# A hybrid decoder layer on one core: four banks begun ahead, filler dealt anew, late constants held back, the last tile by halves

## The chip, the cores and the metric

The kernel runs on one core of one Trainium2 chip. The metric is the device time of one execution in microseconds (us). TensorE (PE) multiplies, VectorE (DVE), ScalarE (ACT) and GpSimd (POOL) do elementwise work, SyncE (SP), ACT and POOL issue DMAs. L12 is line 12 of the kernel before.

## What is computed

One pre-norm decoder layer, x of 512 tokens by 1024 features in float32:

```python
h = rms_norm(x, g_mix)
qa, ka, va, qb, kb, vb, gl = split(h @ w_in)      # 1024 x 4352
ya = swa_sink_attention(rms(qa), rms(ka), va)     # 8 heads, window 128, banded 128-blocks
yb = rms_norm(diff_attention(rms(qb), rms(kb), vb))  # 4 heads, A1 - lam*A2, causal
mixed = sigmoid(gA) * (ya @ w_br_a) + sigmoid(gB) * (yb @ w_br_b)
x = x + mixed @ w_o
u = causal_dwconv3(rms_norm(x) @ w_up)            # 1024 x 5632
x = x + (silu(u_g) * u_v) @ w_down                # 2816 x 1024
```

Both attentions add a relative-position bias that is looked up from a small table.

## The kernel before, in words

**Products.** Each float32 operand is split into a rounded high part and a remainder, and `mm3` (L170 to L174) makes a product of three matmuls: high x high, one operand's remainder, the other's remainder. One `mm3` of 512 columns is called a step here. Weights come from DRAM in units of 128x1024 (`wall`), in the order of `worder`. `split_unit` (L125 to L133) loads a unit on SP (L128), makes `whi` on ACT (L131) and `wlo` on DVE, or on POOL for the units in `pooled` (L132, L158). `wunit(u)` hands out unit u and has everything up to `AHEAD` = 1 unit further loaded and split. There are three raw, three `whi` and three `wlo` buffers.

**Who sets the order.** PE's order is the order of the program text. ACT, DVE and POOL are ordered by a planner from its own estimate of costs, except in the start (L300 to L332), where ACT and DVE too follow the text. Every engine executes its queue in order.

**Start.** SP loads x in eight slices of 128 features (L257) and the first weight units; ACT makes the high part of each x slice (L286), DVE the remainder (L287). POOL issues three loads of constants that are needed later: `relb` (16 KB) and `oneh` (48 KB), from which `bias_vectors` makes the bias, and the part of `cst` behind column `C_HEAD` (216 KB). PE runs eight warming matmuls (L245), then the q projection slice by slice (L348, then `mm3`).

**Attention with filler.** PE would wait at every turn between scores, softmax and value product, so the list `FILL` deals steps of other products (gates, projections, branch products) from a stream `fs` into the gaps: so many steps at each place. `q`, `k`, `k2` stand around the transposes of q and k; `s1`, `s2`, `s3` in unit i of the window attention, after `swa_score(i)`, `swa_trans(i-1)` and `swa_av(i-2)`; in the differential attention (16 units: 4 heads by 4 blocks) `a` after `diff_score`, `c` after `diff_av` and `b` after `diff_trans`. `diff_rms(h)` (norm of a head's output on DVE and ACT, L754 to L761) runs at unit `r[h]` and `diff_out(h)` (transposes on PE, L767, then L768, L769) at unit `o[h]`, both cut at 16, followed by `d[h]` and `e[h]` steps.

**Branch B and w_o.** `br_b_early` begins the first `EARLY` of eight output chunks of `yb @ w_br_b` with three of their four steps each; each holds a PSUM bank. After the attention the last step of these is done (L875 to L883) and the other chunks are made whole by `full`. `mix` then takes each chunk: DVE adds and multiplies (L868, L869), ACT makes the high part (L871), POOL the remainder (L872). `late` (L847) starts the first two chunks of `mixed @ w_o`, six of eight steps each, then the other two; `wunit(U_WO)` and `wunit(U_WO + 1)` are called there, after all mixes.

**Feed-forward.** 44 chunks of w_up, each followed by `conv` on ACT and DVE (L956 to L971); the down product is done by a seven-product scheme (`product`), whose last product T4 ends in two tiles of 128x512, added to the residual on DVE (L1085) and stored by ACT's queue (L1053).

Of the kernel before, what the change touches and what calls it, by code (L numbers as in the profile page):

```python
# [16 lines left out]
ALU = mybir.AluOpType  # L17
AX = mybir.AxisListType

P = 128  # L20
S = 512
# [24 lines left out]
C_HEAD = C_LAM  # L46
# [5 lines left out]
U_QA, U_KV, U_DA, U_VB, U_DB = 0, 4, 6, 10, 14  # L52
U_BRA = 18
U_GATE = 22
U_BRB = 38
U_WO = 42
U_UP = 50
# [8 lines left out]

FILL = dict(r=[5, 9, 13, 16], o=[6, 10, 14, 16], e=[5, 1, 1, 40], kv=4, up=3, warm=8, q=7, k=19, k2=4,
            s1=[0, 3, 0, 3, 2, 4, 4, 0, 0, 3], s2=[2, 3, 0, 5, 1, 7, 5, 5, 0, 0],  # L70
            s3=[3, 0, 2, 5, 6, 2, 2, 6, 0, 1], p0=4, p1=3, p2=10, ud=6, pd=[8, 9], f=[9, 0],
            a=[6, 1, 7, 8, 10, 2, 0, 5, 0, 2, 7, 3, 6, 0, 0, 5],
            b=[6, 2, 4, 4, 2, 7, 2, 1, 2, 2, 0, 0, 1, 4, 2, 2], c=[3, 0, 0, 0, 2, 0, 0, 0, 2, 1, 0, 0, 1, 0, 0, 0],
            d=[1, 0, 0, 5], v0=4)
AHEAD = 1
EARLY = 5


@with_exitstack
def tile_decoder_layer(ctx: ExitStack, tc: tile.TileContext, x4, wall, cst_d, relb_d, oneh_d, xn_d, out):  # L80
    nc = tc.nc
# [19 lines left out]
    def xg_slot():  # L101
        return slot("xg", 16)
# [10 lines left out]
    def pj():  # L113
        return psum.tile([P, S], F32, tag="ps", name=nm("pj"))

    def at():
        return psum.tile([P, S], F32, tag="ps", name=nm("at"))


    cst = const.tile([P, C_N], F32, name="cst")  # L120
# [4 lines left out]
    def split_unit(i, width, eng):  # L125
        raw = wraw.tile([P, 1024], F32, tag="raw", name=nm("raw"))
        src = wall[i] if i < U_N else tsum[(i - U_N) // 6][(i - U_N) % 6]
        nc.sync.dma_start(raw[:, :width], src[:, :width])  # L128
        hi = whip.tile([P, 1024], F32R, tag="hi", name=nm("whi"))
        lo = whip.tile([P, 1024], F32R, tag="lo", name=nm("wlo"))  # L130
        nc.scalar.activation(hi[:, :width], raw[:, :width], AF.Copy)  # L131
        eng.tensor_tensor(lo[:, :width], raw[:, :width], hi[:, :width].bitcast(F32), ALU.subtract)  # L132
        return hi, lo  # L133
# [21 lines left out]
                                 (U_DB, 4), (U_GATE + 8, 8), (U_BRB, 4), (U_WO, 8), (U_UP, 2 * NF), (U_DN, 0))  # L155
              for i in range(n)]
    worder += [U_DN + 6 * op + u for op in DN_ORDER for u in range(6)]
    pooled = {u + i for u, n in ((U_DA, 4), (U_VB, 4), (U_DB, 4), (U_BRA, 4), (U_GATE, 16), (U_BRB + 3, 1)) for i in range(n)}  # L158
    units = {}
    wnext = [4]  # L160

    def wunit(u):
        while wnext[0] < len(worder) and wnext[0] <= worder.index(u) + AHEAD:
            v = worder[wnext[0]]
            width = 512 if v >= U_DN and (v - U_DN) % 6 == 5 else 1024
            units[v] = split_unit(v, width, nc.gpsimd if v in pooled else nc.vector)
            wnext[0] += 1
        return units.pop(u)

    def mm3(ps, a, b, start, stop, skip=False):  # L170

        nc.tensor.matmul(ps, a[0], b[0], start=start, stop=False, skip_group_check=skip)  # L172
        nc.tensor.matmul(ps, a[0], b[1], start=False, stop=False, skip_group_check=skip)  # L173
        nc.tensor.matmul(ps, a[1], b[0], start=False, stop=stop, skip_group_check=skip)  # L174
# [68 lines left out]
    ps = at()  # L243
    for i in range(FILL["warm"]):
        nc.tensor.matmul(ps, zero[:, :P], zero, start=True, stop=True)  # L245

    nc.scalar.dma_start(cst[:, :C_HEAD], cst_d[:, :C_HEAD])
    relb = at1.tile([N_BUCKETS, P], F32, tag="s", name="relb", bufs=3)
    nc.gpsimd.dma_start(relb, relb_d)
    oneh = at1.tile([N_BUCKETS, TOEP], F32, tag="o", name="oneh", bufs=3)  # L250
    nc.gpsimd.dma_start(oneh, oneh_d)
    xr = []
    for k in range(NK):
        xr.append(g_slot(F32))
# [1 line left out]
    def load_x(k, c=slice(0, S)):  # L256
        nc.sync.dma_start(xr[k][:, c], x4[:, k, c])  # L257
# [23 lines left out]
    def split_x(k, c=slice(0, S)):  # L281
        if c.start == 0:
            xg.append((xg_slot(), xg_slot()))
        h, l = [t[:, c] for t in xg[k]]
        gcol = cst[:, C_GMIX + k:C_GMIX + k + 1]
        nc.scalar.activation(h, xr[k][:, c], AF.Copy, scale=gcol)  # L286
        return nc.vector.scalar_tensor_tensor(l, xr[k][:, c], gcol, h.bitcast(F32), ALU.mult, ALU.subtract)  # L287
# [4 lines left out]
    def load_xnat(i):  # L292
        nc.sync.dma_start(xnat[i], xn_d[2 * i:2 * i + 2].rearrange("t p d -> p t d"))

    def square_xnat(t):
        v = xnat[t // 2][:, t % 2, :]
        return nc.scalar.activation(v, v, AF.Square, accum_out=rsum[:, t:t + 1])

    make_identity(nc, ident)
    start = ExitStack()  # L300
# [21 lines left out]
    for kp in range(1, NK // 2):  # L322
        load_x(2 * kp)
        split_x(2 * kp)
        units[U_QA + kp] = split_unit(U_QA + kp, 1024, nc.vector)
        load_x(2 * kp + 1)
        x_split = split_x(2 * kp + 1)
    for i in range(2):
        load_xnat(i)
    for t in range(NT):  # L330
        square_xnat(t)
    start.close()  # L332
    nc.gpsimd.dma_start(cst[:, C_HEAD:], cst_d[:, C_HEAD:])

    def project(u0, width, banks, lead=False):
# [151 lines left out]
    def cut(w, k):  # L487
        return [w[i][:, k * P:(k + 1) * P] for i in range(2)]
# [26 lines left out]
    class Stream:  # L515
# [18 lines left out]
        def fill(self, n):  # L534
            while n > 0 and self.step():
                n -= 1
# [7 lines left out]
    def fill(name, i=None):  # L544
        fs.fill(FILL[name] if i is None else FILL[name][i])

# [229 lines left out]
    def brb_unit(c):  # L776
        if c // 2 not in wb:
            wb[c // 2] = wunit(U_BRB + c // 2)
        return wb[c // 2]
# [3 lines left out]
    def br_b_early():  # L783
        for c in range(EARLY):
            w = brb_unit(c)
            ps = pj()
            for k in range(3):
                mm3(ps, cut(w, 4 * (c % 2) + k), yb[k], start=k == 0, stop=False)
                yield
            brb_banks.append((ps, w))  # L790
# [13 lines left out]
    for i in range(len(todo) + 1):  # L804
        if i < len(todo):
            h, b = todo[i]
            if i == FILL["ud"]:
                fs.until("db")
            for h1 in (2, 3):
                if i == FILL["pd"][h1 - 2]:  # L810
                    qkt[h1] = diff_parts(zt[2], h1 - 2)
# [3 lines left out]
        if i > 0:  # L815
            for u, hb in enumerate(todo):
                if u < len(todo) - 1 and max(u + 2, FILL["v0"]) == i:
                    fs.until("vb")
# [4 lines left out]
            if i == len(todo):  # L823
                diff_av(*todo[-1])
        for step, at_unit in ((diff_rms, FILL["r"]), (diff_out, FILL["o"])):
            for h1 in range(4):
# [19 lines left out]

    def late(u0, grp, cuts, xs, evac):  # L847

        ws = [wunit(u0 + c) for c in range(grp)]
        banks = [pj() for _ in range(grp)]  # L850
        for k0, k1 in zip(cuts, cuts[1:]):
            for ps, w in zip(banks, ws):
                for k in range(k0, k1):
                    mm3(ps, cut(w, k), xs[k], start=k == 0, stop=k == NK - 1)
        for c, ps in enumerate(banks):
            evac(c, ps)

    def full(c, w, off, nk, xs, evac):
        ps = pj()
        for k in range(nk):  # L860
            mm3(ps, cut(w, off + k), xs[k], start=k == 0, stop=k == nk - 1)
        evac(c, ps)
# [13 lines left out]
    for c, (ps, _) in enumerate(brb_banks):  # L876
        for part in last[c]:
            nc.tensor.matmul(ps, part, yb[3][0], start=False, stop=False)
    for c in range(EARLY, 8):
        brb_unit(c)  # L880
    for c, (ps, _) in enumerate(brb_banks):
        nc.tensor.matmul(ps, last[c][0], yb[3][1], start=False, stop=True)
        mix(c, ps)  # L883
    for c in range(EARLY, 8):
        full(c, brb_unit(c), 4 * (c % 2), 4, yb, mix)


# [87 lines left out]
    steps = [(op, u) for op in DN_ORDER for u in range(6)]  # L975
# [12 lines left out]
    first = []  # L988
    for c in range(2):
        w = wunit(U_UP + c)  # L990
# [40 lines left out]
    def product(op, banks, first):  # L1031

        n0 = steps.index((op, 0))
        for u in range(6):
            n = n0 + u
            w = wunit(U_DN + 6 * op + u)
            if n + 1 < len(steps) and n > 0:
                split_left(n + 1)
            a = lefts.pop(n)
            for t in range(2):  # L1040
                for j in range(2 if u < 5 else 1):
                    mm3(banks[t], [a[i][:, 256 * j + P * t:256 * j + P * t + P] for i in range(2)],
                        [w[i][:, 512 * j:512 * j + 512] for i in range(2)],
                        start=first and u == 0 and j == 0, stop=u == 5, skip=not first)
            if op == DN_ORDER[0] and u > 0:
                for i in range(8 * (u - 1) // 5, 8 * u // 5):
                    x1_natural(i // 2, i % 2)
# [4 lines left out]
    def store(i, j, t, v):  # L1052
        nc.scalar.dma_start(out[(2 * i + t) * P:(2 * i + t + 1) * P, j * S:(j + 1) * S], v)  # L1053

    chain, n5 = [at(), at()], [at(), at()]
    product(R11, chain, True)
    p1, us, n5s, ws = [], [], [], []
# [11 lines left out]
    p2 = [at(), at()]  # L1069
# [12 lines left out]
    product(T4, chain, False)  # L1082
    for t in range(2):
        v = x1n[2 * (2 + t)]
        nc.vector.tensor_tensor(v, chain[t], v, ALU.add)  # L1085
        store(1, 0, t, v)


def _bucket_onehot():
# [82 lines left out]
```

## Time and profile before

| | |
|---|---|
| median of 3 runs | 712.83 us |
| lowest, highest | 712.62, 714.18 us |
| the profiled execution: its time | 711.81 us |
| its span, first to last instruction | 710.0 us |
| mean granted TensorE clock | 0.995 |
| PE busy | 690.0 us (97%) |
| DVE, ACT, POOL busy | 486.1, 371.3, 196.8 us |

The profiled execution is 1.8 us longer than its span, and 1.0 us shorter than the median. A row of a timeline gives start, length, engine, line, operation, tiles and, in brackets, the idle time of that engine before it and what ended it.

### The profile page before, as it was taken

The numbers are of one execution on the slowest core, as the hardware profiler recorded it, in microseconds if no ns is written. First come the engines' busy times: TensorE is split into PE (matmuls) and PEld (weight loads), VectorE is DVE, ScalarE is ACT, GpSimd is POOL, SyncE is SP. The second block draws the span as 40 slices with busy tenths as digits, with TensorE's granted clock in tenths as the row PEclk, the third lists the DMA queues.
The fourth block names the chain that finished last, engine by engine and source line by source line (L and its number), as shares of the span: only waits on it lengthen the run. The fifth ranks groups of instructions, "written<-read, shape, count | busy, mean of one in ns | idle before, by whom it ended". The sixth has DMA issues, their size and how long they took to land.

```text
span 710.0 us, 9146 instructions
## 1 busy us (share of the span) xinstructions
PE 690.0 (97%) x3220; PEld 568.2 (80%) x3220; DVE 486.1 (68%) x978; ACT 371.3 (52%) x690; POOL 196.8 (28%) x168
## 2 busy tenths in 40 slices
PE   7999999999999989989999999999999999999997
PEld 5897888778888867768888788888888888888886
DVE  5686786567517787585438868777767677788783
ACT  5537777865336867434325344343334334766661
POOL 2144254533347310283300514332123120100000
PEclk9999999999999999999999999999999999999999
DMA  8672112112232211035422896997986432566773
GB/s 306 260 267 90 60 60 90 59 60 90 70 109 69 80 60 61 30 108 163 144 90 79 281 297 190 324 292 196 266 237 158 138 107 87 162 192 188 228 219 107
DMA packets 28493, 107.86 MB, mean 152 GB/s; under 512 B 3652, under 2 KB 3936, under 8 KB 27936
## 3 DMA queue, kind: packets, MB, share of 16 engines
q1 hardware_dynamic: 21568, 73.67, 31.0%
q0 software_dynamic: 4816, 18.92, 11.9%
q10 hardware_dynamic: 2064, 14.70, 5.5%
q8 instruction: 25, 0.41, 0.2%
q14 instruction: 20, 0.16, 0.1%
HBM read 105.16 MB, written 29.64 MB: 190 GB/s over the span
## 4 chain that ended last, share of the span: by engine, by line
PE 87%; DVE 5%; ACT 5%; issue 1%; DMA 1%; SPq 0%; ACTq 0%; DVEq 0%
PE pj L174 22%; PE pj L172 22%; PE pj L173 22%; PE at L173 5%; PE at L174 5%; PE at L172 5%; DVE g L869 1%; PE at L472 1%; PE at L471 1%; DMA g<-in_x_dram 1%; DVE wlo L132 1%; PE at L626 1%; ACT p L711 1%; DVE g L868 1%; PE at L442 1%
## 5 line engine op out<-in xcount | busy, mean ns | idle before, releaser
L131 ACT ACTIVATE whi<-raw 128x1024 fp32r<-128x1024 f32 x135 | 139.4, 1035 | 152.7 <-PE pj L173 99.1
L172 PE MATMUL pj<-xg,whi 128*128 128x512 f32 x480 | 189.5, 395 | 0.0
L174 PE MATMUL pj<-xg,wlo 128*128 128x512 f32 x480 | 187.7, 391 | 1.2 <-DVE wlo L132 1.2
L173 PE MATMUL pj<-xg,whi 128*128 128x512 f32 x480 | 187.6, 391 | 0.0
L132 DVE TENSOR_TENSOR wlo<-raw,whi 128x1024 fp32r<-128x1024 f32 x102 | 124.8, 1226 | 35.5 <-ACT whi L131 35.0
L132 POOL TENSOR_TENSOR wlo<-raw,whi 128x1024 fp32r<-128x1024 f32 x33 | 79.4, 2411 | 113.8 <-ACT whi L131 108.2
L174 PEld LDWEIGHTS pj<-xg,wlo 128*128 128x128 f32 x480 | 90.4, 188 | 20.6 <-DVE wlo L132 1.7
L172 PEld LDWEIGHTS pj<-xg,whi 128*128 128x128 f32 x480 | 90.5, 189 | 18.1 <-ACT whi L131 0.4
L173 PEld LDWEIGHTS pj<-xg,whi 128*128 128x128 f32 x480 | 90.4, 188 | 17.9
L172 PE MATMUL pj<-whi,xg 128*128 128x512 f32 (+1 forms) x156 | 59.2, 379 | 1.8 <-ACT xg L286 1.8
L956 DVE TENSOR_TENSOR u<-pj,rbc 128x512 f32<-128x512 f32 x44 | 30.2, 689 | 42.2 <-PE pj L174 42.1
L174 PE MATMUL pj<-whi,xg 128*128 128x512 f32 (+1 forms) x156 | 58.3, 374 | 0.1
L173 PE MATMUL pj<-wlo,xg 128*128 128x512 f32 (+1 forms) x156 | 58.0, 372 | 0.0
L172 PE MATMUL at<-whi,xg 128*128 128x512 f32 x146 | 57.3, 393 | 0.0
L174 PE MATMUL at<-whi,xg 128*128 128x512 f32 x146 | 57.0, 390 | 0.0
L173 PE MATMUL at<-wlo,xg 128*128 128x512 f32 x146 | 56.9, 390 | 0.0
L959 ACT ACTIVATE yc<-u,cst 128x512 f32<-128x512 f32 x44 | 35.3, 806 | 9.4 <-DVE u L956 9.1
L963 DVE SCALAR_TENSOR_TENSOR yc<-u,cst,yc 128x511 f32<-128x511 f32 x44 | 35.6, 810 | 2.9 <-ACT yc L959 2.9
L969 ACT ACTIVATE yc<-yc 128x512 f32<-128x512 f32 x22 | 13.9, 632 | 44.6 <-DVE yc L964 44.2
L172 PEld LDWEIGHTS pj<-whi,xg 128*128 128x128 f32 x156 | 29.9, 192 | 7.0 <-ACT xg L286 2.2
L964 DVE SCALAR_TENSOR_TENSOR yc<-u,cst,yc 128x510 f32<-128x510 f32 x44 | 34.1, 777 | 1.3
L174 PEld LDWEIGHTS pj<-whi,xg 128*128 128x128 f32 x156 | 29.8, 191 | 5.7 <-DVE xg L287 0.5
(251 smaller groups left out, 1152.0 us busy)
## 6 DMA issues: line engine op xcount, KB each, us to landing
raw<-in_w_dram SPq DMA_DIRECT2D x108, 512.0 KB, 3.4
tsum<-in_w_dram POOLq DMA_DIRECT2D x24, 512.0 KB, 11.8
raw<-tsum SPq DMA_DIRECT2D x20, 512.0 KB, 3.7
tsum<-in_w_dram ACTq DMA_DIRECT2D x12, 512.0 KB, 6.9
tsum<-tsum ACTq DMA_DIRECT2D x12, 512.0 KB, 6.4
scr<-scr POOLq DMA_DIRECT2D x1, 2304.0 KB, 11.3
xnat<-in_xn_dram SPq DMA_DIRECT2D x2, 1024.0 KB, 9.4
tmp<-in_x_dram POOLq DMA_DIRECT2D x8, 256.0 KB, 3.3
```

The source lines that it names most:

```text
L131: nc.scalar.activation(hi[:, :width], raw[:, :width], AF.Copy)
L132: eng.tensor_tensor(lo[:, :width], raw[:, :width], hi[:, :width].bitcast(F32), ALU.subtract)
L172: nc.tensor.matmul(ps, a[0], b[0], start=start, stop=False, skip_group_check=skip)
L173: nc.tensor.matmul(ps, a[0], b[1], start=False, stop=False, skip_group_check=skip)
L174: nc.tensor.matmul(ps, a[1], b[0], start=False, stop=stop, skip_group_check=skip)
L442: nc.tensor.transpose(ps[:, t * P:(t + 1) * P], zs[t][:, c0:c0 + P], ident)
L471: nc.tensor.matmul(ps, q[:, qsl], kh[:, ksl], start=True, stop=False)
L956: nc.vector.tensor_tensor(u, ps, rbc2, ALU.mult)
L959: i = nc.scalar.activation(y, u, AF.Identity, bias=cst[:, C_CB + ch:C_CB + ch + 1], scale=cw[2])
L963: nc.vector.scalar_tensor_tensor(y[:, 1:S], u[:, 0:S - 1], cw[1], y[:, 1:S], ALU.mult, ALU.add)
L964: nc.vector.scalar_tensor_tensor(y[:, 2:S], u[:, 0:S - 2], cw[0], y[:, 2:S], ALU.mult, ALU.add)
L969: nc.scalar.activation(yg, yg, AF.Silu)
```

## The change

It sets `EARLY` to 4, deals the filler anew, moves `diff_out(1)` from unit 10 to unit 12, makes DVE split `U_BRB + 3` and POOL split `U_UP + 4` to `U_UP + 6`, has the three POOL loads of constants wait for a DVE memset that stands after the split of x slice 3, takes `wunit(U_WO)` (and with it the load and split of `U_WO + 1`) before chunk 6 of branch B, and computes, adds and stores the very last tile in two halves of 256 columns, the second on SP's queue.

```diff
-FILL = dict(r=[5, 9, 13, 16], o=[6, 10, 14, 16], e=[5, 1, 1, 40], kv=4, up=3, warm=8, q=7, k=19, k2=4,
-            s1=[0, 3, 0, 3, 2, 4, 4, 0, 0, 3], s2=[2, 3, 0, 5, 1, 7, 5, 5, 0, 0],
-            s3=[3, 0, 2, 5, 6, 2, 2, 6, 0, 1], p0=4, p1=3, p2=10, ud=6, pd=[8, 9], f=[9, 0],
-            a=[6, 1, 7, 8, 10, 2, 0, 5, 0, 2, 7, 3, 6, 0, 0, 5],
-            b=[6, 2, 4, 4, 2, 7, 2, 1, 2, 2, 0, 0, 1, 4, 2, 2], c=[3, 0, 0, 0, 2, 0, 0, 0, 2, 1, 0, 0, 1, 0, 0, 0],
-            d=[1, 0, 0, 5], v0=4)
+FILL = dict(r=[5, 9, 13, 17], o=[6, 12, 14, 17], e=[5, 0, 2, 40], kv=4, up=3, warm=8, q=7, k=17, k2=7,
+            s1=[2, 0, 0, 3, 2, 2, 3, 0, 11, 3], s2=[0, 4, 0, 4, 1, 1, 5, 5, 2, 0],
+            s3=[5, 1, 2, 4, 8, 3, 6, 6, 0, 1], p0=4, p1=1, p2=10, ud=6, pd=[8, 9], f=[11, 0],
+            a=[6, 1, 6, 8, 10, 2, 0, 4, 1, 1, 7, 2, 6, 0, 4, 5],
+            b=[6, 0, 5, 6, 4, 7, 0, 1, 2, 1, 0, 1, 3, 5, 1, 1], c=[6, 0, 0, 0, 2, 0, 0, 0, 2, 1, 0, 3, 3, 0, 0, 0],
+            d=[0, 1, 4, 5], v0=4)
-EARLY = 5
+EARLY = 4
...
-    pooled = {... (U_GATE, 16), (U_BRB + 3, 1)) ...}
+    pooled = {... (U_GATE, 16), (U_UP + 4, 3)) ...}
...
-    nc.gpsimd.dma_start(relb, relb_d)
-    nc.gpsimd.dma_start(oneh, oneh_d)
...
         x_split = split_x(2 * kp + 1)
+        if kp == 1:
+            for t in (relb[:, 0:1], oneh[:, 0:1], cst[:, C_HEAD:C_HEAD + 1]):
+                nc.vector.memset(t, 0.0)
...
     start.close()
+    nc.gpsimd.dma_start(relb, relb_d)
+    nc.gpsimd.dma_start(oneh, oneh_d)
     nc.gpsimd.dma_start(cst[:, C_HEAD:], cst_d[:, C_HEAD:])
...
-        ws = [wunit(u0 + c) for c in range(grp)]
+        ws = [wo_first if c == 0 else wunit(u0 + c) for c in range(grp)]
...
     for c in range(EARLY, 8):
+        if c == 6:
+            wo_first = wunit(U_WO)
         full(c, brb_unit(c), 4 * (c % 2), 4, yb, mix)
...
-                for j in range(2 if u < 5 else 1):
-                    mm3(banks[t], ...)
+                for c in ((0, S),) if n + 1 < len(steps) or t == 0 else ((0, S // 2), (S // 2, S)):
+                    for j in range(2 if u < 5 else 1):
+                        mm3(banks[t][:, c[0]:c[1]], ...)
...
-        nc.vector.tensor_tensor(v, chain[t], v, ALU.add)
-        store(1, 0, t, v)
+        for c in (slice(0, S),) if t == 0 else (slice(0, S // 2), slice(S // 2, S)):
+            nc.vector.tensor_tensor(v[:, c], chain[t][:, c], v[:, c], ALU.add)
+            (nc.scalar if c.start == 0 else nc.sync).dma_start(out[(2 + t) * P:(3 + t) * P, c], v[:, c])
```

## Rows read from the trace of the kernel before

**Rows 1.** The page, part 1: busy time, share of the span, instructions.

```profile
PE 690.0 (97%) x3220; PEld 568.2 (80%) x3220; DVE 486.1 (68%) x978; ACT 371.3 (52%) x690; POOL 196.8 (28%) x168
```

**Rows 2.** Windows: length, PE, PEld, DVE, ACT, POOL busy (count), granted clock, DMA.

```profile
10.88:14.28 3.40, 3.40 (x9) 2.63 (x10) 2.52 (x4) 2.81 (x4) 0.00 (x0) 0.50 1.05 410
14.30:17.70 3.40, 3.40 (x17) 2.77 (x16) 3.15 (x5) 2.96 (x5) 0.00 (x0) 1.00 1.03 406
256.64:260.04 3.40, 3.40 (x10) 2.63 (x9) 2.69 (x9) 2.24 (x6) 0.00 (x0) 0.50 0.00 0
...
423.42:439.74 16.32, 16.32 (x73) 13.52 (x72) 11.49 (x14) 6.57 (x8) 8.39 (x9) 1.00 0.65 183
```

**Rows 3.** Waits of PE, whole span: total us, times, longest.

```profile
PE at L767 <- ACT o L761: 4.2, 3, 2.5
PE pj L174 <- DVE wlo L132: 2.3, 2, 1.2
...
PE pj L173 <- POOL qv L872: 1.5, 2, 0.7
PE at L727 <- DVE p L717: 1.3, 1, 1.3
...
PE at L472 <- DVE qv L467: 0.8, 1, 0.8
```

**Rows 4.** Timeline around 9 us, ACT and PE.

```profile
9.16 1.40 ACT L286 ACTIVATE xg<-g,cst 128x512 fp32r<-128x512 f32 x2 [2.12 <-DMA g<-in_x_dram]
...
9.93 0.50 PE L172 MATMUL pj<-whi,xg 128*128 128x512 f32 x1 [1.79 <-ACT xg L286]
```

**Rows 5.** Timeline: unit 10's last score, `diff_out(1)`, unit 9's copy, its value product.

```profile
244.91 0.34 PE L472 MATMUL at<-qv,qv 128*128 128x384 f32 x1
...
255.76 0.44 PE L767 MATMUL at<-ident,o 128*128 128x128 f32 x2 [2.46 <-ACT o L761]
...
256.58 0.37 ACT L728 ACTIVATE ath<-at 128x256 fp32r<-128x256 f32 x1
...
261.60 0.41 PE L743 MATMUL at<-vb,ath 128*128 128x256 f32 x2
```

**Rows 6.** Windows of the start, same columns; the last is GB/s.

```profile
5.00:7.00 2.00, 1.89 (x8) 1.57 (x9) 1.17 (x3) 1.05 (x3) 0.00 (x0) 1.00 0.81 188
...
9.00:11.00 2.00, 1.02 (x3) 0.58 (x4) 1.09 (x2) 1.40 (x2) 0.00 (x0) 0.97 1.04 411
```

**Rows 7.** DMA issues of the first 12 us: count, KB each, us to landing.

```profile
cst<-in_c_dram POOLq DMA_DIRECT2D x1, 216.0 KB, 6.2
```

**Rows 8.** Timeline of PE: `diff_out(3)` and the first closing matmul.

```profile
293.10 0.73 PE L767 MATMUL at<-ident,o 128*128 128x128 f32 x4 [0.46 <-ACT o L761]
...
294.61 0.50 PE L878 MATMUL pj<-y,whi 128*128 128x512 f32 x1
```

**Rows 9.** Timeline: softmax of unit 15 (DVE) and its transposes (PE).

```profile
285.38 0.75 DVE L717 SCALAR_TENSOR_TENSOR p<-p,drc 128x512 f32<-128x512 f32 x1
...
286.27 0.63 PE L727 MATMUL at<-ident,p 128*128 128x128 f32 x4
```

**Rows 10.** Timelines of POOL, DVE, PE: mixing, and the start of w_o.

```profile
298.81 2.77 POOL L132 TENSOR_TENSOR wlo<-raw,whi 128x1024 fp32r<-128x1024 f32 x1 [3.27 <-ACT whi L131]
...
299.24 2.89 DVE L869 TENSOR_TENSOR g<-g,g 128x512 f32<-128x512 f32 x1
...
315.19 0.50 PE L174 MATMUL pj<-qv,wlo 128*128 128x512 f32 x1 [1.10 <-DVE wlo L132]
```

**Rows 11.** Timeline: chunk 8 of w_up, DVE and PE.

```profile
400.10 0.69 DVE L956 TENSOR_TENSOR u<-pj,rbc 128x512 f32<-128x512 f32 x1 [0.40 <-PE pj L174]
...
400.71 1.22 DVE L132 TENSOR_TENSOR wlo<-raw,whi 128x1024 fp32r<-128x1024 f32 x1
...
401.98 0.50 PE L174 MATMUL pj<-xg,wlo 128*128 128x512 f32 x1 [1.23 <-DVE wlo L132]
```

**Rows 12.** Timeline of DVE: the last two tiles.

```profile
705.50 1.37 DVE L1085 TENSOR_TENSOR xg<-at,xg 128x512 f32<-128x512 f32 x2 [4.76 <-PE at L174]
```

More of the change, by code (lines that the diff above doesn't have):

```diff
@@ L157, in tile_decoder_layer @@
     worder += [U_DN + 6 * op + u for op in DN_ORDER for u in range(6)]
-    pooled = {u + i for u, n in ((U_DA, 4), (U_VB, 4), (U_DB, 4), (U_BRA, 4), (U_GATE, 16), (U_BRB + 3, 1)) for i in range(n)}
+    pooled = {u + i for u, n in ((U_DA, 4), (U_VB, 4), (U_DB, 4), (U_BRA, 4), (U_GATE, 16), (U_UP + 4, 3)) for i in range(n)}
     units = {}
@@ L1040, in product @@
             for t in range(2):
-                for j in range(2 if u < 5 else 1):
-                    mm3(banks[t], [a[i][:, 256 * j + P * t:256 * j + P * t + P] for i in range(2)],
-                        [w[i][:, 512 * j:512 * j + 512] for i in range(2)],
-                        start=first and u == 0 and j == 0, stop=u == 5, skip=not first)
+                for c in ((0, S),) if n + 1 < len(steps) or t == 0 else ((0, S // 2), (S // 2, S)):
+                    for j in range(2 if u < 5 else 1):
+                        mm3(banks[t][:, c[0]:c[1]], [a[i][:, 256 * j + P * t:256 * j + P * t + P] for i in range(2)],
+                            [w[i][:, 512 * j + c[0]:512 * j + c[1]] for i in range(2)],
+                            start=first and u == 0 and j == 0, stop=u == 5, skip=not first)
             if op == DN_ORDER[0] and u > 0:
```

## The prediction

> **What bounds the kernel now.** I read the page first: PE is busy 690.0 of 710.0 us [rows 1]. Matmuls follow each other every 16.32 / 72 = 0.227 us in a stretch without waits [rows 2], so a step of three takes 0.68 us. The change leaves PE's work as it is, so it can only win where PE waits or runs slowly. Next, therefore, PE's waits [rows 3]: five kinds hold 10.1 us, and a sixth, 1.79 us, stands at 9.93 us [rows 4]. Last, the clock: twice the granted clock is 0.50 for 3.4 us, the lower of its two levels (1.2 instead of 2.4 GHz), and 9 matmuls start where 17 do at 1.00 [rows 2]. Each costs half of 3.4, 1.7 us. The reader should see what came before each: the 1.79 us wait at 9.93, the 2.46 us wait at 255.76 [rows 5]. After waits of 1.3 us and less [rows 3] the clock did not fall. So a long wait costs 1.7 us more than its row says.
>
> **The sum, part by part.** It is made against the profiled execution, 711.81 us, which lies 1.0 us under the median.
>
> *A, constants held back.* PE stops for x slice 1, whose copy starts at 9.16 on landing [rows 4]. Between 5 and 7 us the DMAs move 188 GB/s, between 9 and 11 us 411 [rows 6]; in the slow stretch POOL's `cst` (216 KB, 6.2 us to land [rows 7]) and `oneh` (48 KB) travel beside it. Without them 2 x (411 - 188) = 0.45 MB more pass, 1.1 us at 411 GB/s, and 0.28 MB less are in the way, 0.7 us: slice 1 lands near 7.3, its copy (0.7) ends at 8.0, and PE is free at 9.93 - 1.79 = 8.14. The wait goes, and with it the clock's fall: -3.5. The lower bound of the gain is bytes alone, 0.7; the upper is 3.5. I take 3.5, since the nearest row, 411 GB/s, is what the queue does as soon as POOL's loads are in. What was late next, slice 2, weight unit 1 and slice 3, is 1 MB more (2.5 us), lands by 9.8, and its first part is wanted at 8.14 + 12 x 0.227 = 10.9. What is moved: three memsets of one column on DVE, beside its waits for ACT's copies, and three DMAs on POOL's queue, which now stand behind a wait for DVE at some 12 us (an estimate: that 9.8 and the splits). Nothing urgent is behind them on POOL. Who waits for them is `bias_vectors`, whose matmul PE reaches at 8.14 + 60 x 0.227 = 21.8; with the 6.2 us of `cst` they land by 20. Cost nothing, hidden by this 2 us; uncovered, one for one.
>
> *B, `k2` 4 to 7, `k` 19 to 17.* PE waits 0.8 us for the remainder of k (L472) [rows 3]. Three more steps, 2.0 us, stand between its transpose and the first score. The two steps fewer ahead of the transpose find k normalised long before. -0.8 (bounds 0.5 and 0.8).
>
> *C, `diff_out(1)` from unit 10 to 12.* Its 2.46 us wait and the clock's fall behind it go: -4.2. At its new place some ten steps more lie between norm and transposes. But what covered `diff_av(9)` goes too. Unit 10's last score ends at 245.25, the copy that `diff_av(9)` reads at 256.95 [rows 5]: 11.7 us, because on ACT that copy stands behind unit 10's exponentials. PE reached `diff_av(9)` 16.35 us after that score. Take off 2.46 (wait), 1.7 (clock), 0.5 (transposes), and three steps (15 become 12; 2.04): 9.66. A wait of 2.04 comes up if the chain stays; nothing if ACT's order changes. `d[1]` = 1 puts a step between `diff_rms(1)` and that score, a start of 0.68 for the norm that is in the chain; I take 2.04 - 0.68 = 1.4, nearer to the row. C is -2.8.
>
> *D, `diff_out(2)`.* The L767 waits are 4.2 in three [rows 3]; less 2.46 and 0.46 [rows 5, 8], its own is 1.3. Between `diff_av(11)` and it stand 9 steps, not 6: 2.0 us. -1.3 (bounds 1.0 and 1.7, with two small waits beside it).
>
> *E, new waits at the end of attention.* `b[14]` falls from 2 to 1: the softmax of unit 15 ends at 286.13 and its transposes start at 286.27 [rows 9], so a step taken away there shows as 0.5 us, and the two last value products lose one each: +0.7 (bounds 0 and 1.4). With `EARLY` 4 branch B has 12 early steps, spent exactly before `diff_out(3)`. Before, one step, 0.68, ran while ACT copied its result: `diff_out(3)` ended at 293.83, L878 began at 294.61 [rows 8]. Now PE idles there: +0.7.
>
> *F, mixing.* PE waits for POOL's remainders (1.5) and, at 315.19, for the remainder of `U_WO + 1` (1.1) [rows 3, 10]. DVE's L869 took 2.89 us because POOL's 2.77 us split of `U_BRB + 3` ran to 301.58 [rows 10]; it ended 0.55 after that. With that split on DVE, POOL starts its eight remainders 2.8 us less burdened, and w_o starts 3 steps, 2.0 us, later after the first mix, since chunk 4 is made whole in front of it. The waits, none over 0.7, lie inside 2.0. `U_WO + 1`'s load and split come two chunks (16 steps) sooner on SP, ACT and DVE; queued behind its split are mixes 6 and 7, 1.2 us later, wanted 24 matmuls after w_o's start. -2.6 (bounds 1.0 and 3.1).
>
> The Trainium skill, "SBUF — State Buffer", section "Who interferes with whom", says that a DVE instruction with two SBUF inputs and a GpSimd instruction that reads SBUF exclude each other for a whole instruction. The 2.89 us row agrees. By that rule POOL's three new splits would take time from DVE's `conv`: G would be a loss of 1.6 and the sum -8.1 instead of -10.5.
>
> *G, `U_UP + 4` to `+ 6` on POOL.* PE waits 1.23 us at chunk 8 of w_up for a remainder that DVE made behind L956, which itself had waited for PE [rows 11]. Taking one 1.22 us split [rows 11] out of the crowded stretch lets the planner put that remainder earlier: at most 1.2 won. If the order stays, nothing; if POOL's split (2.8 [rows 10]) holds DVE up by what it exceeds 1.2, 1.6 lost. I take -0.8: freed DVE time brings the remainder to 0.4 before full cover.
>
> *H, last tile by halves.* Two additions of 0.69 [rows 12] become one and two half ones, with one more start; the last store carries half the bytes and has its own queue. -0.1 (bounds -0.4 and +0.3).
>
> Filler elsewhere is dealt so that the wait at L727 (1.3 [rows 3]) keeps its seven steps: no change. `r` and `o` at 17 are cut at 16 as before.
>
> Sum: -3.5 - 0.8 - 2.8 - 1.3 + 1.4 - 2.6 - 0.8 - 0.1 = -10.5; 711.8 becomes 701.3, the median 702.3.
>
> **Rivals.** *The wait moves to `diff_av(9)`* in full, 2.04 us, and the clock falls as it did after 1.79: 3.7 instead of 1.4, 704.6. For it: the chain of 11.7 us has the same producers; against it: the planner orders ACT anew. 0.17.
>
> *POOL's loads cost only their bytes.* Slice 1 then lands 0.7 sooner, a wait of 1.1 remains, and the clock, as after 1.3, stays: 703.4. For it: nothing in the trace proves that 188 GB/s was their doing. The Trainium skill, "DMA: Bandwidth & Descriptors", section "Queues, rings and completion order", has the engines go round between queues packet by packet, which points this way. 0.13.
>
> *G does not do what it should,* the order on DVE staying: 703.1, or 704.7 with POOL in the way. 0.15.
>
> *Slower:* the held-back constants come too late. PE's queue holds the bias matmul, so all behind it stops; every us after 21.8 costs one. It decides when it eats the whole 10.5, at a landing past 32 us, 18 after the issue, three times the 6.2 us that `cst` takes [rows 7]. 0.05.
>
> **How the numbers follow.** My case 0.45, the three rivals 0.45, slower 0.05, near nothing (several of these at once) 0.05. Best case of the bounds: C without a new wait (1.4), E nil in its first half (0.7), F and G full (0.9), H (0.3): 699.0. Two rivals together give 705 to 706, with F at its lower bound 707. So 698.9 to 707.0. A change under 0.2%, 1.4 us, can't be told from none: the three runs spread by that. Faster 0.91, same 0.04, slower 0.05.
>
> **What would show it.** Right: no wait over 0.3 at the second x slice and clock 1.00 from 5 us on; L767 waits under 1 in total; a new wait before L878 near 0.8; no wait for L872; the last PE matmul some 10 us sooner. Wrong: 188 GB/s still at 5 us; a wait at L743 of unit 9 with clock 0.50 behind it; a PE wait at L272; a 1.2 us wait left in w_up.

## The result, and the profile after

The median falls from 712.83 to 704.72 us (three runs, 704.37 to 705.58): a ratio of 0.989, interval 0.987 to 0.992. The prediction was 702.3, in a range of 698.9 to 707.0. Put beside the kernel before once more, in six runs on another chip, the kernel after stood at 704.80 against 710.72: 0.9916 (0.9901 to 0.993), a gain of 5.9 us. The profiled execution of after took 705.58 us; its span, 703.8, is 6.2 shorter than that of before.

The first part of the page of after, busy times as in [rows 1]:

```profile
PE 688.3 (98%) x3223; PEld 569.4 (81%) x3223; DVE 482.9 (69%) x980; ACT 371.3 (53%) x690; POOL 201.0 (29%) x170
```

PE's work is the same, so the gain is waiting. To see where, I cut both spans at the same four instructions of PE: the first transpose of q (L442 before, L446 after), the first `diff_trans` (L727, L731), the first closing matmul of branch B (L878, L882), the first matmul of w_up. The windows view of before, columns as in [rows 2]:

```profile
0.00:48.60 48.60, 44.94 (x226) 36.15 (x226) 31.77 (x84) 23.82 (x37) 14.10 (x19) 0.96 0.80 288
48.60:151.59 102.99, 99.43 (x511) 82.76 (x509) 70.84 (x209) 79.16 (x181) 44.32 (x34) 1.00 0.22 74
151.59:294.61 143.02, 138.29 (x683) 114.86 (x683) 91.54 (x292) 83.44 (x202) 44.89 (x25) 0.99 0.21 71
294.61:354.89 60.28, 57.27 (x244) 45.26 (x244) 38.55 (x41) 24.23 (x34) 31.48 (x23) 1.00 0.40 131
354.89:706.14 351.25, 350.02 (x1561) 289.20 (x1559) 252.62 (x354) 160.68 (x238) 62.01 (x68) 1.00 0.65 193
```

And of after: the same five, then the start that answers to [rows 6], then two stretches of which more below:

```profile
0.00:46.26 46.26, 43.97 (x225) 35.05 (x226) 32.11 (x86) 23.80 (x37) 13.92 (x19) 1.00 0.83 298
46.26:147.55 101.29, 99.08 (x511) 82.78 (x509) 72.05 (x210) 78.70 (x181) 44.55 (x35) 1.00 0.23 77
147.55:289.95 142.40, 137.30 (x674) 114.84 (x674) 91.26 (x292) 83.54 (x202) 44.97 (x25) 0.98 0.21 72
289.95:348.47 58.52, 58.14 (x252) 47.29 (x253) 36.42 (x42) 24.42 (x34) 28.34 (x22) 1.00 0.41 135
348.47:699.78 351.31, 349.84 (x1564) 289.42 (x1562) 250.30 (x351) 160.84 (x238) 69.21 (x71) 1.00 0.65 193
...
5.00:7.00 2.00, 2.00 (x9) 1.67 (x10) 0.83 (x3) 0.13 (x1) 0.00 (x0) 1.00 0.84 194
...
254.26:257.66 3.40, 3.40 (x13) 2.84 (x12) 3.29 (x15) 2.41 (x9) 0.00 (x0) 0.50 0.04 11
281.57:284.97 3.40, 3.40 (x14) 2.97 (x13) 0.83 (x2) 1.17 (x4) 0.00 (x0) 0.50 0.00 0
```

The second number is the length, the third PE's busy time; their difference is PE's idle time. The clock fell to its lower level once in stretch 1 and once in stretch 3 before, and twice in stretch 3 after. Nine matmuls (three steps, 2.04 us at 0.227) leave the third stretch for the fourth: that is `EARLY` 4. So the table's prediction for these two has the sum's steps and the 2.04:

| stretch | idle before, after | change of length | predicted |
|---|---|---|---|
| 1, start | 3.7, 2.3 | -2.34 | -3.5 (A) |
| 2, window attention | 3.6, 2.2 | -1.70 | -0.8 (B) |
| 3, third attention | 4.7, 5.1 | -0.62 | -4.7 (C, D, E -2.7; steps -2.0) |
| 4, mixing and w_o | 3.0, 0.4 | -1.76 | -0.6 (F -2.6; steps +2.0) |
| 5, feed-forward | 1.2, 1.5 | +0.06 | -0.8 (G) |
| behind the last matmul | | +0.11 | -0.1 (H) |
| sum | | -6.25 | -10.5 |

The third stretch lost three steps of work and became 0.6 shorter: it waits more than before. Waits of PE in the profile of after (total us, times, longest), which answer to [rows 3]:

```profile
PE at L747 <- ACT ath L732: 2.7, 2, 1.7
PE at L731 <- DVE p L721: 1.7, 2, 1.3
PE pj L174 <- DVE wlo L132: 1.5, 1, 1.5
...
PE pj L172 <- ACT xg L284: 1.0, 1, 1.0
PE at L731 <- DVE dnmx L713: 0.8, 1, 0.8
PE pj L882 <- ACT y L772: 0.8, 1, 0.8
...
PE pj L173 <- POOL act L876: 0.4, 1, 0.4
PE at L750 <- DVE atl L733: 0.2, 1, 0.2
PE at L771 <- ACT o L765: 0.2, 1, 0.2
```

The 4.2 us of `diff_out` are 0.2 now. In their place stand L747 (1.75 at `diff_av(9)`, 0.99 at `diff_av(14)`), the transposes of units 14 and 15 (0.8, 0.35) and the closing matmul (0.8).

### The profile page after: what moved, and what is told of

The parts are those of the page before. It is cut to its first block, busy times and chain, and to the rows that moved or that the text cites. A ratio compares the mean times of both kernels' runs of the same rounds, so it can differ in the third digit from the quotient of the medians.

```text
span 703.8 us, 9155 instructions
## 1 busy us (share of the span) xinstructions
PE 688.3 (98%) x3223; PEld 569.4 (81%) x3223; DVE 482.9 (69%) x980; ACT 371.3 (53%) x690; POOL 201.0 (29%) x170
## 4 chain that ended last, share of the span: by engine, by line
PE 86%; ACT 5%; DVE 4%; POOL 1%; DMA 1%; issue 1%; SPq 0%; DVEq 0%; ACTq 0%
PE pj L172 22%; PE pj L174 22%; PE pj L173 22%; PE at L174 5%; PE at L172 5%; PE at L173 5%; POOL qv L876 1%; ACT p L715 1%; PE at L476 1%; PE at L475 1%; DMA g<-in_x_dram 1%; PE at L630 1%; PE at L446 1%; DMA tsum<-in_w_dram 1%; ACT whi L131 1%
## 5 line engine op out<-in xcount | busy, mean ns | idle before, releaser
L132 DVE TENSOR_TENSOR wlo<-raw,whi 128x1024 fp32r<-128x1024 f32 x100 | 121.1, 1213 | 36.5 <-ACT whi L131 36.0
L132 POOL TENSOR_TENSOR wlo<-raw,whi 128x1024 fp32r<-128x1024 f32 x35 | 84.0, 2406 | 128.6 <-ACT whi L131 115.3
L172 PE MATMUL pj<-whi,xg 128*128 128x512 f32 (+1 forms) x156 | 58.3, 374 | 1.0 <-ACT xg L284 1.0
L174 PE MATMUL pj<-whi,xg 128*128 128x512 f32 (+1 forms) x156 | 57.6, 369 | 0.1
```

## The experiments

All are timed against the kernel before on the same chip. "After" below is its second comparison:

> The kernel after, unchanged, beside the same runs of the kernel before as the other three: what their own difference is taken against. Theory (what the traces of the first pair of runs show is the change's own): 0.989 of the kernel before, within the interval of 0.987 to 0.992 of its first run. Rival (part of the first difference belongs to the chip of that day; the four kernels tried since, each next to the kernel after, stood at 0.991 to 0.992): 0.991 to 0.993.

Measured: 0.9916, so the rival's figure, at the edge of the first interval. Experiments are read against 0.9916, and stretch by stretch in their profiles.

**What the clock does.** In the six runs of after the mean granted clock and the time go together: 703.88 and 704.05 us at 1.000, 704.73 to 705.12 at 0.998, 706.40 at 0.995. The profiled one of these had no fall to the lower level. The timelines at `diff_av(9)`, of after's first profile:

```profile
252.59 0.50 PE L747 MATMUL at<-vb,ath 128*128 128x256 f32 x2 [1.75 <-ACT ath L732]
```

and of its second:

```profile
253.02 0.50 PE L747 MATMUL at<-vb,ath 128*128 128x256 f32 x2 [1.72 <-ACT ath L732]
```

The same wait; behind the first the clock is 0.50 from 254.26, behind the second it stays (windows of the second profile, the stretch of the same work, and the whole third stretch):

```profile
254.79:258.19 3.40, 3.40 (x20) 2.96 (x19) 3.20 (x15) 2.41 (x9) 0.00 (x0) 1.00 0.10 13
...
148.01:288.27 140.26, 134.89 (x673) 112.27 (x673) 91.16 (x292) 83.41 (x202) 44.90 (x25) 1.00 0.22 73
```

13 matmuls instead of 20 start in 3.4 us: a fall costs 7/20 of 3.4, 1.2 us here, and may or may not come. So stretches are compared below at equal numbers of falls.

**A undone and A alone.**

```diff
+    nc.gpsimd.dma_start(relb, relb_d)
+    nc.gpsimd.dma_start(oneh, oneh_d)
...
-            for t in (relb[:, 0:1], oneh[:, 0:1], cst[:, C_HEAD:C_HEAD + 1]):
-                nc.vector.memset(t, 0.0)
...
-    nc.gpsimd.dma_start(relb, relb_d)
-    nc.gpsimd.dma_start(oneh, oneh_d)
```

> The kernel after, with the three loads of constants back at their old place on POOL's queue and without the three memsets; nothing else. Theory (their bytes alone stand in the way of the first operands; from the two traces the start up to zqT is 2.33 us shorter after): the time rises by 2.0 to 2.6, to 706.7 to 707.3, and the shift is there at zqT already. Rival 1, the prediction's step A (the slow packets at 4 to 7 us are theirs): +3.5, 708.2. Rival 2 (the start is shorter for another reason, the order of the warming and first score matmuls for instance): within 0.5 of 704.7.

Measured: 705.97 us, 0.9922 (0.9902 to 0.9942), 0.0006 or 0.4 us above after. The theory's size fell, and so did step A's. In its profile the wait at the second x slice is back, but the clock stays at 1.00 behind it (timeline, to be held against [rows 4]):

```profile
9.70 0.50 PE L172 MATMUL pj<-whi,xg 128*128 128x512 f32 x1 [1.78 <-ACT xg L286]
```

The reverse, the same lines put into the kernel before:

> The kernel before with A alone: the three loads of constants held back behind the last square, and the three memsets of one column. Theory (the start of one kernel differs from execution to execution by the pace of single packets and of the clock's rise: PE reached its first window-attention transpose at 83.10 in the one and 84.26 in the other profile of the same code, and with the constants early in the kernel after at 83.17 against 81.7 to 82.9 in five with them late): 0.3 to 1.2 faster than before, 0.998 to 0.9995. Rival 1, the prediction's step A: -3.5, 0.995. Rival 2, the first pair of traces: -2.3, 0.9968.

Measured: 710.79, 0.9999 (0.9981 to 1.0016), in twelve runs of 708.94 to 715.44. In the median no gain is measurable. But the runs fall into two groups: six lie between 708.94 and 709.89, below every one of the seventeen runs of the kernel before beside them (710.32 at the least), and six at 711.68 or more. The profile is of the second group. Its first stretch is 2.5 us shorter than before's (46.06), but the second 107.25 instead of 102.99, through a fall of the clock and two waits at the first score (windows, and waits of PE):

```profile
46.06:153.31 107.25, 102.53 (x511) 85.06 (x510) 72.03 (x211) 79.31 (x181) 46.83 (x36) 0.97 0.23 80
...
PE at L475 <- ACT qv L469: 1.3, 1, 1.3
...
PE at L476 <- DVE qv L471: 1.2, 1, 1.2
```

Over all profiles of this study the first stretch took 47.4 to 48.6 us in three with early constants (mean 47.8) and 45.8 to 47.2 in eleven with late ones (mean 46.3). That is 1.5 less, but the 48.6, of the kernel before, holds a fall of the clock; the two early ones without a fall, 47.45 and 47.43, are 1.1 above the mean of the late ones. So A gives about 1.1 there, and what follows can take it back.

**C undone: `diff_out(1)` back at unit 10.**

```diff
-FILL = dict(r=[5, 9, 13, 17], o=[6, 12, 14, 17], ...
+FILL = dict(r=[5, 9, 13, 17], o=[6, 10, 14, 17], ...
```

> The kernel after, with diff_out(1) back from unit 12 to unit 10 of the third attention (list o, second number). Theory (the chain of DVE and ACT through dnmx, p and ath is late there as a whole, so the wait changes its place only): a wait of 2 to 2.5 us with a fall of the clock at diff_out(1), none at diff_av(9), and a time within 1.0 of 704.7. Rival, the prediction's step C as it was made (diff_out(1) later takes out 2.8 net): 2.8 slower, 707.5, with the wait at diff_av(9) there as well.

Measured: 706.10, 0.9923 (0.9904 to 0.9943), 0.5 us above after. The theory holds, with a wait of 2.75 where it said 2 to 2.5: one wait at the old place (waits of PE), none at `diff_av(9)`, and the clock falls behind it. The third stretch follows (windows).

```profile
PE at L771 <- ACT o L765: 2.8, 1, 2.8
...
148.47:291.55 143.08, 137.16 (x674) 114.66 (x674) 91.82 (x292) 83.59 (x202) 44.96 (x25) 0.98 0.22 72
```

The third stretch, 143.08, has two falls, as the 142.40 of after. Moving `diff_out(1)` moves the wait.

**Filler for `diff_av(9)`.**

```diff
-a=[6, 1, 6, 8, 10, 2, 0, 4, 1, 1, 7, 2, 6, 0, 4, 5],
+a=[6, 1, 6, 8, 10, 2, 0, 4, 1, 1, 7, 5, 3, 0, 4, 5],
```

> The kernel after, with three filler steps of unit 12 of the third attention dealt to unit 11, ahead of diff_av(9) (list a: 2, 6 become 5, 3). Theory (PE is three steps of filler short before ath is there, and the clock falls for the pause): the waits of 1.75 and 0.25 us at diff_av(9) go, and the 3.4 us at the half clock behind them with 1.7 us lost: -3.4 to -4.0, 700.7 to 701.3. Rival 1 (the same wait stands behind the next product that needs the chain, as three steps fewer are left there): a new wait of about 2 us at dtrans or diff_av of units 12 to 13, and a time within 1.0 of 704.7. Rival 2 (only the wait goes, the fall of the clock comes with the later waits anyway, and lasts): -2.0, 702.7.

Measured: 705.67, 0.992 (0.9904 to 0.9937). Rival 1: the wait stands one unit on, at `diff_av(10)`, with 2.04 us (timeline, and the third stretch in windows):

```profile
259.50 0.62 PE L747 MATMUL at<-vb,ath 128*128 128x256 f32 x3 [2.04 <-ACT ath L732]
...
147.67:290.17 142.50, 136.72 (x674) 113.50 (x674) 91.39 (x292) 83.56 (x202) 44.92 (x25) 0.99 0.22 72
```

With `d=[0, 1, 4, 5]` made `[0, 1, 0, 5]` besides:

> As the run with three steps sooner, and three more filler steps moved from before dscore14's products to behind them (list d, third number 4 to 0 ... the steps then stand in the end). Theory (what waits at dtrans14, diff_av(14) and dtrans15 is the softmax behind dscore14, which starts sooner when fewer steps stand before it, and has more steps to hide it): the waits of 0.79, 0.99 and 0.35 us and the clock's fall at 281.6 go: another -2.5 to -3.8, 697.0 to 698.5. Rival (the steps fail where they stood and the wait comes at diff_out(3) or the first mixing, at 0.2 and 0.78 us now): as the run before it or up to 2 slower.

Measured: 705.01, 0.9913 (0.9895 to 0.9931), no gain of 2.5. The waits of 0.79 and 0.99 at unit 14 go, the 2.04 at `diff_av(10)` stays, and branch B's early steps now wait for `diff_out(2)` (timeline, and the third stretch):

```profile
275.35 0.50 PE L172 MATMUL pj<-y,whi 128*128 128x512 f32 x1 [0.81 <-ACT y L772]
276.13 0.50 PE L173 MATMUL pj<-y,whi 128*128 128x512 f32 x1 [0.29 <-DVE y L773]
...
147.27:289.18 141.91, 136.88 (x673) 113.50 (x673) 91.42 (x292) 83.62 (x202) 44.96 (x25) 0.99 0.22 72
```

**Filler from where there is slack.** Softmax results of units 5 and 6 lie ready for 20 and 6 us in the profile of after.

```diff
-e=[5, 0, 2, 40] ... pd=[8, 9], f=[11, 0],
+e=[6, 0, 2, 40] ... pd=[7, 9], f=[0, 0],
-a=[..., 2, 0, 4, 1, 1, 7, 2, 6, 0, 4, 5], b=[..., 1, 3, 5, 1, 1],
+a=[..., 2, 0, 9, 1, 1, 7, 5, 6, 0, 4, 4], b=[..., 1, 3, 5, 2, 1],
```

> The kernel after with filler taken from where PE's transposes find their softmax long ready (6 to 20 us at units 5 to 7) to where they wait: the third attention's q and k parts of head 2 made one unit sooner (pd 8 to 7) with no filler behind them (f 11 to 0), one step to before them (e 5 to 6), five of them behind unit 7's score (a 4 to 9), three before diff_av(9) (a 2 to 5), the rest left over for unit 14, and one moved from unit 15's score to between dtrans14 and diff_av(14) (a 5 to 4, b 1 to 2). Theory (PE is short of cover after unit 9, not short in all): the waits of 1.72 and 0.25 at diff_av(9) and of 0.8 and 0.99 at units 14 and 15 fall to under 1.2 together, with their two falls of the clock: -2.5 to -5.0 against the kernel after, 0.985 to 0.988 of before. Rival (DVE and ACT, busy 9 of 10 us from 235 to 255, can't start sooner, and unit 8's chain with the earlier q and k parts in front of it is late in its turn): waits of 1 to 2.5 us at dscore8, diff_av(7) or dtrans8 in their place, within 1.0 of the kernel after.

Measured: 704.16, 0.9904 (0.9889 to 0.9918); its four runs lie between 704.03 and 704.26, with a clock of 0.999 or more in each. The rival holds for the length: the waits at `diff_av(9)` are gone, others stand at `diff_av(6)`, `diff_av(11)` and unit 14 (waits of PE), and the third stretch (windows) is 140.7 us, not under after's 140.26 without falls.

```profile
PE at L747 <- ACT ath L732: 2.0, 3, 0.9
...
PE at L731 <- DVE dnmx L713: 1.5, 1, 1.5
...
147.71:288.42 140.71, 135.62 (x673) 112.30 (x673) 90.38 (x292) 83.65 (x202) 44.87 (x25) 1.00 0.21 73
```

> As the run that took filler from the slack, with single steps set before the four waits that it left, 0.78, 0.89, 1.50 and 0.31 us: one between dtrans6 and dscore8 (a 9 to 8, b 0 to 1), one between unit 13's score and diff_av(11) (c 3 to 2, a 0 to 1), four from before unit 14's score to behind it (d 4 to 0, a 4 to 5), and none behind diff_out(2) (e 2 to 0, the first steps of branch B then stand behind unit 15's score). Theory (each wait is a lack of so many steps at its place, and the softmax of unit 14 ends as much sooner as its score starts): the four fall to under 1.2 in total, 0.3 to 0.8 of them at dtrans15; -1.5 to -2.7 against that run, 701.4 to 702.7, 0.9866 to 0.9883 of before, and no fall of the clock. Rival (DVE and ACT carry unit 14's chain no sooner, being at unit 13's and at the norm before diff_out(2)): the 1.50 stays or moves to diff_out(2) or dtrans15, within 0.7 of that run.

Measured: 704.03, 0.99 (0.9884 to 0.9917), four runs within 704.01 to 704.07. Again the rival: the 1.50 moves to `diff_out(2)` (1.09) and `diff_av(14)` (0.71), and the stretch (windows) is no shorter:

```profile
147.58:288.38 140.80, 136.54 (x674) 111.96 (x674) 90.64 (x292) 83.25 (x202) 44.88 (x25) 1.00 0.22 73
```

Its idle time is 4.3 us, that of after's second profile 5.4; but PE's busy time for the same matmuls at the same clock is 1.65 longer. That several waits too short to show as idle replace a few long ones fits this, and is not shown. Both kernels are as fast as the best runs of after (703.88, 704.05), and more even; that their median is better is not shown, the intervals overlap.

**F alone, on the kernel before.**

```diff
-EARLY = 5
+EARLY = 4
-    ... (U_GATE, 16), (U_BRB + 3, 1)) ...
+    ... (U_GATE, 16)) ...
-        ws = [wunit(u0 + c) for c in range(grp)]
+        ws = [wo_first if c == 0 else wunit(u0 + c) for c in range(grp)]
...
+        if c == 6:
+            wo_first = wunit(U_WO)
```

> The kernel before with F and nothing else: four banks begun ahead instead of five, the last unit of branch B split on DVE instead of POOL, w_o's first weight unit two chunks sooner. Theory (the two traces: -3.8 between the last block of attention and w_o's third chunk, +0.8 for the new wait at the first mixing): -2.5 to -3.5 against before. Rival 1 (the prediction: -2.6 and +0.7): -1.9. Rival 2 (the waits of POOL's remainders and of the second unit of w_o appear again later in w_o): within 1.0 of before.

Measured: 711.02, 0.9992 (0.998 to 1.0004): nothing in the median. At an equal clock there is a gain: 708.78 and 709.21 us at 0.998, against 710.14 to 710.78 of the kernel before on the same chip, and 710.44 to 711.06 at 0.995, against 711.60 to 712.41, so 1.0 to 1.5. But five of its twelve runs have a clock of 0.993 or less, and none of the seventeen of before. All three expectations had the place wrong; only the size of rival 2 came true. The waits of mixing are gone, but the third attention lost three steps and became longer. The fourth stretch, too, holds a fall of the clock that before's has not (0.97). Windows of the two:

```profile
150.46:294.12 143.66, 135.66 (x674) 113.42 (x674) 91.69 (x292) 83.37 (x202) 44.89 (x25) 0.99 0.22 71
294.12:354.05 59.93, 59.58 (x252) 48.34 (x253) 36.43 (x42) 24.40 (x34) 28.28 (x22) 0.97 0.41 132
```

and its waits of PE, to be held against [rows 3]:

```profile
PE at L767 <- ACT o L761: 5.5, 3, 2.5
...
PE pj L878 <- ACT y L768: 0.8, 1, 0.8
```

1.4 more at `diff_out(3)` and 0.8 more at L878: the three steps that branch B no longer has there. The rest stands at the value product of unit 11 (1.09 and 0.50): here the clock did not fall behind the 2.46 us wait at `diff_out(1)`, PE came sooner, and waited for ACT instead, with a fall behind these (timeline):

```profile
267.71 0.74 PE L743 MATMUL at<-vb,ath 128*128 128x256 f32 x4 [1.09 <-ACT ath L728]
```

**`EARLY` alone, in the kernel after.**

```diff
-EARLY = 4
+EARLY = 5
```

> The kernel after with five banks begun ahead again instead of four (EARLY 4 to 5), all else as after. F alone on the kernel before took the waits for POOL's remainders away and still gave nothing, 0.9992, as waits of 0.88 us more at diff_av(9), 0.49 behind it, 1.36 more at diff_out(3) and 0.7 more at the first mixing came up. Theory (the three steps of branch B that the fourth bank gives up, 2.0 us, were what covered the end of attention; what is won in the mixing is what is taken from there): the waits at diff_out(3) and at the first mixing, 0.47 and 0.78, go, waits for POOL's remainders of 0.7 to 1.5 come back in w_o, and the time is within 0.8 of the kernel after. Rival 1 (three splits of branch B on POOL were what made those waits, and EARLY has nothing to do with it): no waits in w_o, 1.2 to 2.0 faster than the kernel after. Rival 2 (the prediction's step F lies in EARLY): 1.5 to 2.5 slower.

Measured: 706.83, 0.9944 (0.9928 to 0.996), 0.0028 or 2.0 us above after; rival 2 has the size, the theory the places but for `diff_out(3)`, which keeps its 0.47. (The waits that this expectation puts at `diff_av(9)` of F alone stand at `diff_av(11)`.) The profile, without a fall, has waits for POOL back; its third and fourth stretch follow:

```profile
PE pj L173 <- POOL act L876: 1.3, 1, 1.3
...
PE pj L173 <- POOL qv L876: 1.0, 2, 0.7
...
148.28:289.68 141.40, 136.84 (x682) 114.06 (x683) 91.88 (x292) 83.38 (x202) 45.83 (x26) 1.00 0.21 72
289.68:348.51 58.83, 56.53 (x244) 45.34 (x243) 35.70 (x41) 24.32 (x34) 27.34 (x20) 1.00 0.40 134
```

Its stretches against after's second profile, also without a fall, are 141.40 to 140.26 and 58.83 to 58.52; together they are 1.45 longer: `EARLY` 4 is worth 1.45 us under the new deal. From the kernel before, with the same work, the fourth stretch falls from 60.28 to 58.83: the rest of F is worth 1.45 too, if nothing else of the change acts there.

**G and H undone.**

```diff
-    ... (U_GATE, 16), (U_UP + 4, 3)) ...
+    ... (U_GATE, 16)) ...
```

> The kernel after without G: the remainders of the three units U_UP+4 to +6 on DVE again. Theory (a wait of 1.46 us at chunk 9 of w_up stands after where 1.23 stood at chunk 8 before, with DVE's copies of the moved sums in front of the remainder): no change, within 0.7 of the kernel after in the same runs, and the wait back at chunk 8 or 9 with 1.2 to 1.5. Rival 1, the prediction's step G: 0.8 slower. Rival 2 (DVE, POOL and the shared SBUF inputs: the three splits on POOL hold DVE up): 0.5 to 1.6 faster.

Measured: 705.43, 0.9921 (0.9906 to 0.9935). The theory: the fifth stretch is 351.31 with and without G. Its wait (timeline)

```profile
396.15 0.50 PE L174 MATMUL pj<-xg,wlo 128*128 128x512 f32 x1 [1.02 <-DVE wlo L132]
```

stands a chunk sooner than after's 1.46 at 401.01, with a 0.16 before it. POOL's splits did hold up one small operation of DVE, which took 2.24 us beside them in the first profile of after and 0.16 without them; PE waited for it in neither. Timelines of DVE, after and without G:

```profile
367.07 2.24 DVE L215 TENSOR_TENSOR coll<-y,colh 128x4 f32<-128x4 f32 x1
...
368.71 0.16 DVE L215 TENSOR_TENSOR coll<-y,colh 128x4 f32<-128x4 f32 x1
```

H undone is the last tile whole, as in the kernel before:

> The kernel after without H: the last tile added and stored whole, as before. Theory (from the last matmul to the end of the span it was 3.90 us before and 4.02 after: what the half addition wins, the start of another store takes): within 0.4 of the kernel after, with 3.9 us behind the last matmul. Rival (the halves do win, and other things made the end longer): 0.4 to 0.7 slower than the kernel after, and 4.4 or more behind the last matmul.

Measured: 705.21, 0.9914 (0.9898 to 0.9931); 3.90 us behind the last matmul instead of 4.02 to 4.03. The theory: the halves give nothing, or lose 0.1.

## Why the prediction was right, and where it was not

The time fell within the range, by the mechanism "PE can only win where it waits". The sum was 4.3 us too good against the profiled execution. After's median is 0.9 below its profiled execution, whose clock fell twice, and the prediction had added 1.0: the medians differ by 2.4.

That the time lies within the range is in part luck. The upper end of the range stood for two rivals at once, and all three came in some part: bytes only (A), the wait at `diff_av(9)` with a fall of the clock (C), and nothing from G; B and F won more than was said. The kernel before also stood at 712.83 in its first three runs, against medians of 710.64 to 711.08 beside the experiments: of the 10.5 us predicted the first pair shows 8.1 and the second comparison 5.9. Three of the four signs of being wrong came: 194 GB/s at 5 us, the wait at the value product of unit 9 with the clock at 0.50 behind it, and a wait in w_up, of 1.46.

**A** failed on its cause: "Without them 2 x (411 - 188) = 0.45 MB more pass". Without POOL's loads the DMAs move 194 GB/s from 5 to 7 us, against 188 [rows 6]; in all profiles it is 186 to 257 with late constants and 188 to 221 with early ones. The loads did not make that stretch slow; what did stays open. The wait at the second x slice stays at 1.0 of 1.79. The rival "only their bytes" has the right kind, 2.3 of its 2.4 in the first pair of profiles. But 1.7 of its 2.4 is the clock, and with early constants in the kernel after the clock did not fall behind a wait of 1.78; at equal falls 1.1 is left.

**B** was right where it named the wait (0.8, gone); the other 0.9 of its stretch, 0.49 of it a wait at L626 that is gone, is put down to the new `s` lists, which the sum called "no change". No run tried them alone.

**C, D and E** are the failed step, 4.1 of the 4.3; in after's second profile, without a fall, the third stretch is 140.26 and the miss 1.9. "I take 2.04 - 0.68 = 1.4" left a short wait at `diff_av(9)` with no fall of the clock. It came with 1.75 and 0.25, and the clock fell in this execution: the first rival. From unit 10's last score to the end of the copy that `diff_av(9)` reads it is 11.3 us instead of 11.7, so the earlier start of the norm gave 0.4 at most and not 0.68. D's wait is gone from `diff_out(2)`, as said, but E looked for the next late thing at units 14 and 15 and gave it 0.7; there are 2.1 us, and a second fall. (Eight steps stand before `diff_out(2)`, not nine.) What the sum missed is common to C, D and E: it followed the cover of each wait by itself, not the chain through the whole stretch. Six deals of the filler (after, `diff_out(1)` at 10, three sooner, six moved, and the two from the slack) give the third stretch 140.3, 143.1, 142.5, 141.9, 140.7 and 140.8 us with 0, 2, 1, 1, 0 and 0 falls; at 1.2 each taken off, all lie within 140.3 to 141.3. Shown is that a wait filled at one place comes up at the next; that DVE and ACT's chain through `dnmx`, `p` and `ath` sets the length is argued from what the waits end on, and no run made that chain shorter.

E's other part is right: 0.78 at L882, predicted 0.7.

**F** won more than was said, and its link was missed. The fourth stretch is 3.8 shorter at equal work (-1.76 less 2.04) for 2.6 predicted and 3.1 as the upper bound; of the waits for POOL's remainders one of 0.4 is left. But E charged the three steps that `EARLY` 4 takes from attention with 0.7 only. On the old deal their waits, and the falls of the clock behind these, cost as much as F won in the median (0.9992), and left 1.0 to 1.5 at an equal clock; under the new deal `EARLY` 4 alone is worth 1.45.

**G** gave nothing: "Taking one 1.22 us split out of the crowded stretch lets the planner put that remainder earlier" did not happen; the third rival. The rule of the Trainium skill that was weighed there ("SBUF — State Buffer", section "Who interferes with whom") would have made a loss of 1.6, and that did not come either: 351.31 against 351.25. A DVE operation was held up (L215, 2.24 us instead of 0.16), off PE's path. **H** was nothing, +0.1.

The rival on the slow side did not come: the three loads, issued at 13.5 to 14.7, landed at 18.6 to 20.8 us, and PE, at the bias matmul (L272 before, L270 after) at 23.4, waits for none of them. The prediction's issue "at some 12" does not go with its landing "by 20" and its 18 us before 32; both take an issue at 14.

## What to carry to other kernels

Filler that only changes places moves a wait; before counting a wait as gone, find what else those steps covered, and take off what it will cost there. Count a change that takes work out of a stretch (here: banks begun ahead) in both stretches. And compare kernels that differ by a few us at equal numbers of clock falls, in the same stretches between the same instructions, before believing a part's worth.

## What had not been expected of the hardware

**A DVE operation of 8 columns that takes 5 us.** The two waits behind A alone seem to begin in the norm of k. DVE and POOL in that kernel's timeline:

```profile
42.82 4.97 DVE L431 TENSOR_TENSOR hv<-ss,r2tok 128x8 f32<-128x8 f32 x1
...
43.02 4.73 POOL L132 TENSOR_TENSOR wlo<-raw,whi 128x1024 fp32r<-128x1024 f32 x2
```

and in the last of the filler deals, with the DVE operation behind it:

```profile
40.94 4.75 POOL L132 TENSOR_TENSOR wlo<-raw,whi 128x1024 fp32r<-128x1024 f32 x2
...
42.98 0.38 DVE L431 TENSOR_TENSOR hv<-ss,r2tok 128x8 f32<-128x8 f32 x1
43.39 2.33 DVE L432 TENSOR_SCALAR hv<-hv 128x8 f32<-128x8 f32 x1
```

The first ends at 47.79, POOL's second split at 47.75. In all fourteen profiles this operation ends within 0.05 us of the end of one of the two splits: after 0.4 us where it comes just before the gap between them, after 2.9 to 5.0 where it must await the second. PE waits at the first score in the kernels with the new `k2` where it ends at 47.15 or later (0.66, 1.16), and not where it ends at 46.6 or sooner; of these two, the one that ends 0.52 later, counted from its first transpose of q, waits 0.50 longer. The Trainium skill, "SBUF — State Buffer", section "Who interferes with whom", has a DVE instruction with two SBUF inputs and a GpSimd instruction that reads SBUF exclude each other; the trace agrees, with 4.97 us for 8 columns here and 2.24 us for the 4 columns of L215 beside G's splits. That in A alone the operation starts 0.20 us before the first split, and still ends with the second, the rule does not explain. So a start that is a us faster can run into a split and give it back. Keeping POOL free there was not tried.

**The clock's fall is not a fixed price of a wait.** The same 1.7 us wait was followed by one in one execution and not in another, and it cost 1.2 us in the third attention, not the 1.7 of the prediction. In the eight runs of the two kernels whose profile shows no wait over 1.5 us in the third attention, the clock stayed at 0.999 or more. But the prediction's "After waits of 1.3 us and less" it "did not fall" holds for its own trace only: in the profile of after the second fall, at 281.57, comes behind waits of 0.79, 0.99 and 0.35 us, and in A alone one of 6.8 us begins at 66.42, behind a wait of 1.29 and within one of 1.16.
